# Stick-breaking logits that alternate between two heads, and cross-attention values in four strips of 128 columns

## The chip, the cores and the metric

The kernel runs on one core of a Trainium2 chip. The metric is the device time of one execution in microseconds (us); less is better. The time of the kernel before is the median of three runs, 981.52 us.

## The reference, cut to what matters

One step of a small streaming encoder with two layers, 256 prompt tokens and 32 sample tokens, 1024 features, 16 heads of 64. Layer 0 mixes eight heads of softmax attention with eight heads of stick-breaking attention; layer 1 has sixteen softmax heads with a forget bias. Each layer then has a cross-attention into 256 memory tokens (4 heads of 256) and a SwiGLU feed-forward part. The change touches the stick-breaking logits and the cross-attention of the sample tokens.

```python
def stick_break_attend(q, k, v, q_pos, k_pos):
    z = jnp.einsum('bqhd,bkhd->bhqk', q, k).astype(jnp.float32) * (HEAD_DIM ** -0.5)
    before = k_pos[None, :] < q_pos[:, None]
    log_keep = jnp.where(before, jax.nn.log_sigmoid(-z), 0.0)
    log_later = lax.cumsum(log_keep, axis=3, reverse=True) - log_keep
    w = jnp.where(before, jnp.exp(jax.nn.log_sigmoid(z) + log_later), 0.0)
    return jnp.einsum('bhqk,bkhd->bqhd', w.astype(v.dtype), v)

def memory_attn(h, mk, mv, w_q, w_o):
    b, t, _ = h.shape
    q = (h @ w_q).reshape(b, t, XA_HEADS, XA_HEAD_DIM)
    s = jnp.einsum('bqhd,bkhd->bhqk', q, mk).astype(jnp.float32) * (XA_HEAD_DIM ** -0.5)
    p = jax.nn.softmax(s, axis=-1)
    o = jnp.einsum('bhqk,bkhd->bqhd', p.astype(mv.dtype), mv)
    return o.reshape(b, t, D_MODEL) @ w_o
```

## The kernel before

All activations stand with features on the 128 partitions and the 288 tokens (256 prompt, 32 sample) in the columns. A weight unit is a 128x1024 block (512 KB). `unit` (L132) loads it from HBM through SP's queue into `st`, makes a high part `hi` on ACT (L141) and the rest `lo` on DVE (L142), and `mm3` (L145) does three TensorE matmuls per 128x128 block with them: 24 per unit. `st` and `lo` have four buffers, `hi` five. These projections (`pj`, `op`, `dn`, `mv` in the trace) fill most of the time.

Attention is written as Python generators. `tick` (L176) advances each active one by a step after every projection, so that the pieces of attention lie between projections on TensorE, and the work of ACT and DVE for them runs beside the next projection. PSUM has four banks for accumulators of projections and four for attention (`att`, L64), each a bank of 128x512 fp32. An engine's instructions run mostly in the order of the source; at some places the framework has set a matmul of one piece between those of another.

The array has 128 rows (the contraction) and 128 columns (the output's partitions). A matmul whose operands stand on partitions 64 to 127 uses the lower row half, one whose output stands on PSUM partitions 32 to 63 the second strip of 32 columns. In the trace, a shape such as 64*128 gives rows and columns of the array that are used; a matmul of two plain fp32 operands leaves two records, its two passes.

The parts that the change touches:

- `stick_prompt` (L459), called for j = 4 to 7 in layer 0. A tile q[j] holds two heads, one in each half of the partitions. For head 0 and then head 1 it computes the logits `zb` in a PSUM bank of the head's own: two q.k matmuls with 64 rows (256 and 128 columns), then two full-array bf16 matmuls of `identb` with `mdiag`, which add the mask. `stick_logs` (L429) takes both banks through Abs, Exp and Ln on ACT and one DVE instruction per head. Three steps later `stick_weights` (L444) multiplies by `ntrir` and `nones` into the same banks.
- `stick_sample` (L480), called twice, for the 32 sample tokens of two tiles: for each head two matmuls with the cache's keys (`ck`, 64 rows, 128 columns of the array), one mask matmul (`msamp`), and two with the new keys (64 rows, 32 columns), into the head's bank `zs`.
- `attend` in `cross` (L626), called twice per layer by `sample` (L621), each time for two of the four heads: logits `xss`, softmax, two transposes `xst`, a DVE copy to `xsw`; then the values `xso`: for two halves kt of the memory and two heads i, a matmul with 32 columns of weights and 256 columns of values, head i on partitions 32i to 32i + 31. DVE copies 64x256 to `xsn`, two transposes of 64x128 put features on the partitions (`xsp`), and four `split_o` (L324; ACT, then DVE) write the output's parts `oh` and `ol`.
- For comparison: `attend_prompt` (L357) computes its logits `sc` for two heads from two row halves, with no mask matmul between; `sample_pv` (L407) computes `os` in four strips of 32 columns.
- Around them: `mem_scales` (L510) runs in the first `Memory.step` (L540) behind the first stick-breaking prompt call: matmuls `nrm`, then the chain on DVE that ends in `y` (L225 to L230), then matmuls `nr`. `head` (L598) is the cross-attention of the prompt (`xs`, `xt`, `xw`, `xo`), and `out_project` (L292) runs the output projection, in which the products that need the last heads come last.

Of the kernel before, what the change touches and what calls it, by code (L numbers as in the profile page):

```python
# [26 lines left out]
def encoder_step(ctx: ExitStack, tc: tile.TileContext, a):  # L27
# [14 lines left out]
    V, S, G, T, DMA = nc.vector, nc.scalar, nc.gpsimd, nc.tensor, nc.sync  # L42
    cnt = [0]

    def name(s):
        cnt[0] += 1
        return f"{s}{cnt[0]}"

    def tok(s, dt=F32):
        return tk.tile([P, NT], dt, tag="t", name=name(s))  # L50

    def work(s):
        return wk.tile([P, 512], F32, tag="w", name=name(s))

    def work2(s, dt=F32):
        return wk.tile([P, 768], dt, tag="w2", bufs=4, name=name(s))
# [7 lines left out]
    def att(s):  # L64
        return ps.tile([P, 512], F32, tag="at", bufs=4, name=name(s))

    def mm(out, lhsT, rhs, start=True, stop=True):
        T.matmul(out, lhsT, rhs, start=start, stop=stop, skip_group_check=True)  # L68
# [54 lines left out]
    ident = cst.tile([P, P], F32, name="ident")  # L123
# [189 lines left out]
    def split(t, hi, lo, eng=G):  # L313
        S.copy(hi, t)
        eng.tensor_tensor(lo, t, hi.bitcast(F32), ALU.subtract)
        return hi, lo
# [7 lines left out]
    def split_o(p, oh, ol):  # L324
        S.copy(oh, p)
        V.tensor_tensor(ol, p, oh.bitcast(F32), ALU.subtract)

    def v_natural(v):
        p = att("vt")
        T.transpose(p[:, 0:128], v[:, 0:128], ident)  # L330
        T.transpose(p[:, 128:256], v[:, 128:256], ident)
        T.transpose(p[0:NS, 256:384], v[:, 256:288], ident)
        vn = wk.tile([P, 384], F32, tag="vn", bufs=5, name=name("vn"))
        S.copy(vn[:, 0:256], p[:, 0:256])
        S.copy(vn[0:NS, 256:384], p[0:NS, 256:384])
        return vn
# [92 lines left out]
    def stick_logs(zs):  # L429

        ab = work2("ab")
        c = 0
        for z, n, _ in zs:
            S.activation(ab[:, c:c + n], z[:, :n], AF.Abs)
            c += n
        S.activation(ab[:, :c], ab[:, :c], AF.Exp, scale=-1.0)
        S.activation(ab[:, :c], ab[:, :c], AF.Ln, bias=1.0)
        c = 0
        for z, n, _ in zs:
            V.scalar_tensor_tensor(ab[:, c:c + n], z[:, :n], 0.0, ab[:, c:c + n], op0=ALU.max, op1=ALU.add)  # L440
            c += n
        return ab

    def stick_weights(zs, sp, parts=None):  # L444

        w = work2("sw")
        c = 0
        for z, n, later in zs:
            if parts:
                mm(z[:, :n], ntrir, parts[0][:, c:c + n], False, False)  # L450
                mm(z[:, :n], ntrir, parts[1][:, c:c + n], False, False)
            else:
                mm(z[:, :n], ntri, sp[:, c:c + n], False, False)
            mm(z[:, later[0]:later[1]], nones, sp[:, c + later[2]:c + later[3]], False, True)
            S.activation(w[:, c:c + n], z[:, :n], AF.Exp)
            c += n
        return w

    def stick_prompt(q, k, v, vns, j, oh, ol):  # L459
        vn = vns[j] = v_natural(v)  # L460
        zs = []
        for hd in range(2):
            r = slice(64 * hd, 64 * hd + 64)
            z = att("zb")

            mm(z[:, 0:256], k[r, 0:128], q[r, 0:256], True, False)
            mm(z[:, 256:384], k[r, 128:256], q[r, 128:256], False, False)
            mm(z[:, 0:128], identb, mdiag, False, False)
            mm(z[:, 256:384], identb, mdiag, False, False)
            zs.append((z, 384, (128, 256, 256, 384)))  # L470
        sp = stick_logs(zs)
        parts = split(sp, work2("sh", F32R), work2("sl", F32R), V)
        yield 1
        yield 1
        yield 1
        w = stick_weights(zs, sp, parts)
        yield 1
        prompt_pv([w[:, 0:384], w[:, 384:768]], vn, oh, ol)

    def stick_sample(qs, ks, two, vns, ck, cv, o):  # L480
        yield 1

        zs = []
        for hd in range(2):
            z = att("zs")
            r = slice(64 * hd, 64 * hd + 64)
            for j in range(2):
                mm(z[:, 32 * j:32 * j + 32], ck[j][r], qs[j][r, 256:288], j == 0, False)
            mm(z[:, 64:128], identb, msamp, False, False)
            for j in range(2):  # L490
                mm(z[0:NS, 64 + 32 * j:96 + 32 * j], ks[j][r, 256:288], qs[j][r, 256:288], False, False)
            zs.append((z, 128, (0, 64, 64, 128)))
        sp = stick_logs(zs)
        yield 1
        yield 1
        w = stick_weights(zs, sp)
        yield 1
        yield from sample_pv(w, lambda j, hd: (128 * hd + 32 * j, 128 * hd + 64 + 32 * j), [vns[j] for j in two], cv, o)
# [74 lines left out]
    def cross(layer, cur, memory, nxt):  # L573
        o = ([tok("oh", F32R) for _ in range(KT)], [tok("ol", F32R) for _ in range(KT)])
        q, qs = [], []
# [50 lines left out]
        def attend(g, ck, cv):  # L626
            s = att("xss")
            for i in range(2):
                for f in range(2):
                    mm(s[32 * i:32 * i + 32, 0:256], qs[4 * g + 2 * i + f][:, 256:288], ck[i][:, 256 * f:256 * f + 256], f == 0, f == 1)  # L630
            e = work("xse")
            softmax(s[0:64], [(0, 256)], None, e[0:64])
            yield 1
            tt = att("xst")
            T.transpose(tt[:, 0:64], e[0:64, 0:128], ident[0:64, 0:64])
            T.transpose(tt[:, 64:128], e[0:64, 128:256], ident[0:64, 0:64])
            w = work("xsw")
            V.tensor_copy(w[:, 0:128], tt[:, 0:128])
            yield 1
            po = att("xso")  # L640
            for kt in range(2):
                for i in range(2):
                    mm(po[32 * i:32 * i + 32, 0:256], w[:, 64 * kt + 32 * i:64 * kt + 32 * i + 32],
                       cv[i][:, 256 * kt:256 * kt + 256], kt == 0, kt == 1)
            t = work("xsn")
            V.tensor_copy(t[0:64, 0:256], po[0:64, 0:256])
            yield 1
            pt = att("xsp")
            for f in range(2):
                T.transpose(pt[:, 64 * f:64 * f + 64], t[0:64, 128 * f:128 * f + 128], ident[0:64, 0:64])  # L650
            for i in range(2):
                for f in range(2):
                    b = 4 * g + 2 * i + f
                    split_o(pt[:, 64 * f + 32 * i:64 * f + 32 * i + 32], o[0][b][:, 256:288], o[1][b][:, 256:288])

        for hd in range(4):
            project_q(hd)
# [288 lines left out]
    r = tok("rf")  # L946
# [87 lines left out]
```

## Time and profile before

| What | Value |
|---|---|
| median of three runs | 981.52 us (979.58 to 983.31) |
| the profiled execution | 981.77 us, of which its span is 979.9 us |
| TensorE matmuls (PE) | 960.9 us busy, 98% of the span |
| weight loads (PEld) | 925.1 us, 94% |
| VectorE (DVE) | 589.5 us, 60% |
| ScalarE (ACT) | 483.8 us, 49% |
| GpSimd (POOL) | 194.6 us, 20% |
| chain of work that ended last | PE 90%, DMA 3%, DVE 3%, issue and ACT 1% each |

The span runs from the first to the last instruction that the profiler saw; the rest of the execution's time lies around it. Busy time of PE is to be read with care: a matmul's record lasts from its start to a modelled end, while the next has often started, so starts tell more than durations. A row of the timeline gives the start, the length from the first start to the last end of a run of like records, the engine, the line, the operation, the tile written and those read, the shape and the number of records. All matmuls but transposes are written by the helper in line 68, so they are told apart by their tiles.

### The profile page before, as it was taken

Reading aid. Unit: us, or ns where it says so; the run is one execution under the profiler, and the core shown is the slowest. Engines: PE = TensorE matmul, PEld = TensorE weight load, DVE = VectorE, ACT = ScalarE, POOL = GpSimd, SP = SyncE. Lnnn points to the kernel's source line nnn. Section 1 sums busy time; section 2 is a strip of 40 time slices with the busy share of each in tenths; the row PEclk is TensorE's granted clock in tenths of the full one; section 3 lists DMA queues with packets and bytes.
Section 4 is the critical chain, followed back from the end, with each engine's and each line's share of the span. In section 5 each row is a group of like instructions: output and inputs, shape, how many; then the busy total and the mean of one; then the engine's idle time right before and its main releaser. Section 6 shows DMA issues by size and latency. Waiting matters only on the chain.

```text
span 979.9 us, 19034 instructions
## 1 busy us (share of the span) xinstructions
PE 960.9 (98%) x7449; PEld 925.1 (94%) x7449; DVE 589.5 (60%) x1135; ACT 483.8 (49%) x854; POOL 194.6 (20%) x293
## 2 busy tenths in 40 slices
PE   8999999999999999999999999999999999999995
PEld 7789999998899999999998999999989999999995
DVE  6686454677676555764565666657757655555452
ACT  5556767555455444444444545445546544444330
POOL 3121001210113222411003234213002222222010
PEclk9999999999999999999999999999999999999997
DMA  7775345544254454455455555545425444444431
GB/s 235 247 248 192 127 165 174 169 168 143 91 179 158 165 173 167 178 193 173 166 201 167 179 191 182 170 160 194 149 100 168 155 159 165 173 164 166 165 109 49
DMA packets 60137, 163.59 MB, mean 167 GB/s; under 512 B 8160, under 2 KB 21520, under 8 KB 60048
## 3 DMA queue, kind: packets, MB, share of 16 engines
q1 hardware_dynamic: 60048, 162.38, 49.0%
q8 instruction: 59, 0.97, 0.4%
q14 instruction: 30, 0.25, 0.1%
HBM read 152.20 MB, written 11.72 MB: 167 GB/s over the span
## 4 chain that ended last, share of the span: by engine, by line
PE 90%; DMA 3%; DVE 3%; issue 1%; ACT 1%; SPq 0%; POOL 0%; DVEq 0%; ACTq 0%; POOLq 0%
PE pj L68 50%; PE dn L68 14%; PE op L68 11%; PE mv L68 5%; DMA st<-w_ab 2%; PE zb L68 1%; PE xs L68 1%; PE xo L68 1%; PE po L68 1%; DVE lo L142 1%; DMA skew<-lined 1%; PE sc L68 1%; PE nr L68 1%; ACT hi L141 1%; PE zs L68 1%
## 5 line engine op out<-in xcount | busy, mean ns | idle before, releaser
L141 ACT CAST hi<-st 128x1024 fp32r<-128x1024 f32 x260 | 272.2, 1049 | 339.4 <-issue 146.9
L68 PE MATMUL pj<-hh,hi 128*128 128x288 f32 (+1 forms) x1352 | 405.1, 300 | 0.0
L68 PE MATMUL pj<-hl,hi 128*128 128x288 f32 (+1 forms) x1352 | 399.8, 296 | 1.7 <-DVE hl L248 1.7
L142 DVE TENSOR_TENSOR lo<-st,hi 128x1024 fp32r<-128x1024 f32 x260 | 323.3, 1244 | 128.8 <-PE dn L68 41.3
L68 PE MATMUL pj<-hh,lo 128*128 128x288 f32 (+1 forms) x1352 | 399.4, 295 | 0.0
L68 PEld LDWEIGHTS pj<-hh,hi 128*128 128x128 f32 x1352 | 256.6, 190 | 6.2 <-issue 4.7
L68 PEld LDWEIGHTS pj<-hl,hi 128*128 128x128 f32 x1352 | 256.5, 190 | 3.3 <-DVE hl L248 3.2
L68 PEld LDWEIGHTS pj<-hh,lo 128*128 128x128 f32 x1352 | 256.7, 190 | 0.0
L68 PE MATMUL dn<-fh,hi 128*128 128x288 f32 x400 | 108.7, 295 | 0.0
L68 PE MATMUL dn<-fh,lo 128*128 128x288 f32 x352 | 103.7, 295 | 0.0
L68 PE MATMUL dn<-fl,hi 128*128 128x288 f32 x304 | 89.5, 294 | 0.0
L68 PE MATMUL op<-ol,hi 128*128 128x288 f32 x256 | 75.5, 296 | 0.0
L68 PE MATMUL op<-oh,lo 128*128 128x288 f32 x256 | 75.5, 295 | 0.0
L68 PE MATMUL op<-oh,hi 128*128 128x288 f32 x256 | 75.1, 296 | 0.0
L68 PEld LDWEIGHTS dn<-fh,hi 128*128 128x128 f32 x400 | 72.5, 188 | 0.0
L68 PEld LDWEIGHTS dn<-fh,lo 128*128 128x128 f32 x352 | 66.1, 188 | 0.0
L213 POOL TENSOR_TENSOR ssq<-ssq,sq 128x288 f32<-128x288 f32 (+1 forms) x37 | 37.0, 1000 | 120.0 <-ACT sq L202 77.8
L68 PEld LDWEIGHTS dn<-fl,hi 128*128 128x128 f32 x304 | 57.1, 188 | 0.0
L691 POOL TENSOR_TENSOR fl<-us,fh 128x288 fp32r<-128x288 f32 x38 | 32.8, 863 | 119.0 <-ACT fh L690 119.0
L686 DVE TENSOR_TENSOR us<-pj,rstd 128x288 f32<-128x288 f32 x44 | 20.1, 457 | 59.4 <-PE pj L68 59.4
L687 POOL TENSOR_TENSOR gs<-gs,sg 128x288 f32<-128x288 f32 x44 | 38.8, 882 | 75.5 <-ACT sg L685 75.5
L68 PEld LDWEIGHTS op<-ol,hi 128*128 128x128 f32 x256 | 48.2, 188 | 0.8 <-issue 0.8
(253 smaller groups left out, 1213.7 us busy)
## 6 DMA issues: line engine op xcount, KB each, us to landing
st<-w_gate SPq DMA_DIRECT2D x44, 512.0 KB, 3.3
st<-w_up SPq DMA_DIRECT2D x44, 512.0 KB, 3.2
st<-w_down SPq DMA_DIRECT2D x44, 512.0 KB, 3.3
st<-w_c SPq DMA_DIRECT2D x25, 512.0 KB, 3.3
st<-w_ab SPq DMA_DIRECT2D x23, 512.0 KB, 4.2
st<-w_xk SPq DMA_DIRECT2D x16, 512.0 KB, 3.6
st<-w_xv SPq DMA_DIRECT2D x16, 512.0 KB, 3.5
st<-w_xq SPq DMA_DIRECT2D x16, 512.0 KB, 4.3
```

Of the source, the lines that this page charges most:

```text
L68: T.matmul(out, lhsT, rhs, start=start, stop=stop, skip_group_check=True)
L141: S.copy(hi[:, b], st[:, b])
L142: V.tensor_tensor(lo[:, b], st[:, b], hi[:, b].bitcast(F32), ALU.subtract)
L213: eng.tensor_tensor(s[:, :self.n], self.acc[i][:, :self.n], q[:, :self.n], ALU.add)
L686: V.tensor_tensor(us, pu[:, :NT], cur.r, ALU.mult)
L687: G.tensor_tensor(gs, gs, sg, ALU.mult)
L691: G.tensor_tensor(lo, us, hi.bitcast(F32), ALU.subtract)
```

## The change

In `stick_prompt` both banks are taken first; the q.k matmuls go column block by column block and alternate between the two heads, which lie on the array's row halves; the mask matmuls of both heads follow. In `stick_sample` the same is done: the matmuls with the cache's keys alternate between the heads, then come both mask matmuls, then those with the new keys, alternating. In `attend` of the cross-attention the values of two heads are computed in four strips of 32 array columns, each with 128 columns of values (head i, half f of its features) where there were two with 256: 16 passes of 128 columns instead of 8 of 256. The copy to `xsn` covers 128x128 instead of 64x256, and one transpose of 128x128 takes the place of two of 64x128. The four `split_o` and their sizes stay.

```diff
--- before.py
+++ after.py
@@ -458,16 +458,17 @@
 
     def stick_prompt(q, k, v, vns, j, oh, ol):
         vn = vns[j] = v_natural(v)
-        zs = []
-        for hd in range(2):
-            r = slice(64 * hd, 64 * hd + 64)
-            z = att("zb")
-
-            mm(z[:, 0:256], k[r, 0:128], q[r, 0:256], True, False)
-            mm(z[:, 256:384], k[r, 128:256], q[r, 128:256], False, False)
+        zz = [att("zb") for _ in range(2)]
+
+
+        for k0, q0, c0, c1 in ((0, 0, 0, 256), (128, 128, 256, 384)):
+            for hd in range(2):
+                r = slice(64 * hd, 64 * hd + 64)
+                mm(zz[hd][:, c0:c1], k[r, k0:k0 + 128], q[r, q0:256], k0 == 0, False)
+        for z in zz:
             mm(z[:, 0:128], identb, mdiag, False, False)
             mm(z[:, 256:384], identb, mdiag, False, False)
-            zs.append((z, 384, (128, 256, 256, 384)))
+        zs = [(z, 384, (128, 256, 256, 384)) for z in zz]
         sp = stick_logs(zs)
         parts = split(sp, work2("sh", F32R), work2("sl", F32R), V)
         yield 1
@@ -480,16 +481,17 @@
     def stick_sample(qs, ks, two, vns, ck, cv, o):
         yield 1
 
-        zs = []
-        for hd in range(2):
-            z = att("zs")
-            r = slice(64 * hd, 64 * hd + 64)
-            for j in range(2):
+        zz = [att("zs") for _ in range(2)]
+        rr = [slice(64 * hd, 64 * hd + 64) for hd in range(2)]
+        for j in range(2):
+            for z, r in zip(zz, rr):
                 mm(z[:, 32 * j:32 * j + 32], ck[j][r], qs[j][r, 256:288], j == 0, False)
+        for z in zz:
             mm(z[:, 64:128], identb, msamp, False, False)
-            for j in range(2):
+        for j in range(2):
+            for z, r in zip(zz, rr):
                 mm(z[0:NS, 64 + 32 * j:96 + 32 * j], ks[j][r, 256:288], qs[j][r, 256:288], False, False)
-            zs.append((z, 128, (0, 64, 64, 128)))
+        zs = [(z, 128, (0, 64, 64, 128)) for z in zz]
         sp = stick_logs(zs)
         yield 1
         yield 1
@@ -638,20 +640,20 @@
             V.tensor_copy(w[:, 0:128], tt[:, 0:128])
             yield 1
             po = att("xso")
+
+            strips = [(i, f, slice(64 * i + 32 * f, 64 * i + 32 * f + 32)) for i in range(2) for f in range(2)]
             for kt in range(2):
-                for i in range(2):
-                    mm(po[32 * i:32 * i + 32, 0:256], w[:, 64 * kt + 32 * i:64 * kt + 32 * i + 32],
-                       cv[i][:, 256 * kt:256 * kt + 256], kt == 0, kt == 1)
+                for i, f, b in strips:
+                    mm(po[b, 0:128], w[:, 64 * kt + 32 * i:64 * kt + 32 * i + 32],
+                       cv[i][:, 256 * kt + 128 * f:256 * kt + 128 * f + 128], kt == 0, kt == 1)
             t = work("xsn")
-            V.tensor_copy(t[0:64, 0:256], po[0:64, 0:256])
+            V.tensor_copy(t[:, 0:128], po[:, 0:128])
             yield 1
             pt = att("xsp")
-            for f in range(2):
-                T.transpose(pt[:, 64 * f:64 * f + 64], t[0:64, 128 * f:128 * f + 128], ident[0:64, 0:64])
-            for i in range(2):
-                for f in range(2):
-                    b = 4 * g + 2 * i + f
-                    split_o(pt[:, 64 * f + 32 * i:64 * f + 32 * i + 32], o[0][b][:, 256:288], o[1][b][:, 256:288])
+            T.transpose(pt[:, 0:128], t[:, 0:128], ident)
+            for i, f, b in strips:
+                m = 4 * g + 2 * i + f
+                split_o(pt[:, b], o[0][m][:, 256:288], o[1][m][:, 256:288])
 
         for hd in range(4):
             project_q(hd)
```

## Rows read from the trace of the kernel before

**Rows 1.** Windows: busy us (instructions) by PE, PEld, DVE, ACT, POOL; clock, DMA.
```profile
84.00:264.00 180.00, 179.86 (x1407) 168.78 (x1406) 106.73 (x204) 108.60 (x194) 20.50 (x22) 1.00 0.44 148
690.00:738.00 48.00, 48.00 (x361) 42.83 (x361) 30.25 (x72) 22.30 (x56) 1.54 (x2) 1.00 0.31 110
```

**Rows 2.** ACT's groups, 84 to 264 us: busy, mean ns | idle before, its releasers.
```profile
L141 ACT CAST hi<-st 128x1024 fp32r<-128x1024 f32 x42 | 43.9, 1047 | 51.5 <-PE pj L68 23.9 <-issue 8.9 <-PE op L68 8.4
```

**Rows 3.** Timeline of PE, first stick-breaking prompt call: start, length (us), instruction.
```profile
84.53 0.27 PE L331 MATMUL vt<-ident,kv 128*128 128x128 f32 x1
84.64 0.27 PE L332 MATMUL vt<-ident,kv 128*32 128x128 f32 x1
84.84 0.92 PE L68 MATMUL zb<-q,kv 64*128 64x256 f32 x4
85.69 0.28 PE L68 MATMUL zb<-mdiag,identb 128*128 128x128 bf16 x2
...
86.76 0.28 PE L68 MATMUL zb<-mdiag,identb 128*128 128x128 bf16 x2
86.88 0.56 PE L68 MATMUL nrm<-mean,ssq 128*128 128x2 f32 x4
```

**Rows 4.** Timeline of PE, logits of a softmax prompt call, both heads.
```profile
27.61 0.93 PE L68 MATMUL sc<-kv,q 64*128 64x128 f32 x8
28.47 0.40 PE L68 MATMUL pj<-hh,hi 128*128 128x288 f32 x1
```

**Rows 5.** Timeline of PE, first stick-breaking sample call, from head 0 to head 1.
```profile
111.07 0.63 PE L68 MATMUL zs<-q,ca 64*128 64x32 f32 x4
111.64 0.20 PE L68 MATMUL zs<-msamp,identb 128*128 128x64 bf16 x1
...
112.01 0.63 PE L68 MATMUL zs<-q,ca 64*128 64x32 f32 x4
```

**Rows 6.** Timeline of PE, values of the cross-attention's first sample.
```profile
233.36 1.06 PE L68 MATMUL xso<-ca,xsw 128*32 128x256 f32 x8
234.35 0.40 PE L68 MATMUL pj<-hh,hi 128*128 128x288 f32 x1
```

**Rows 7.** Timeline of PE, values of a softmax sample in four strips.
```profile
53.16 0.32 PE L68 MATMUL os<-ca,pts 128*32 128x64 f32 x8
53.41 0.31 PE L68 MATMUL os<-vn,pts 32*32 32x64 f32 x8
```

**Rows 8.** Timeline of PE around the transposes of the cross-attention's first sample.
```profile
238.71 0.40 PE L68 MATMUL xo<-xw,vh 128*128 128x256 f32 x2
238.95 0.28 PE L68 MATMUL xo<-xw,vl 128*128 128x256 f32 x1
239.16 0.33 PE L650 MATMUL xsp<-ident,xsn 64*128 64x64 f32 x2
...
239.64 0.29 PE L68 MATMUL xs<-kl,qh 128*128 128x256 f32 x1
```

**Rows 9.** Timelines of DVE, ACT and PE behind the first prompt call.
```profile
86.61 0.19 DVE L326 TENSOR_TENSOR ol<-ot,oh 128x32 fp32r<-128x32 f32 x1 [0.84 <-ACT oh L325]
87.48 0.16 DVE L225 TENSOR_SCALAR ms<-nrm 128x4 f32<-128x4 f32 x1 [0.67 <-PE nrm L68]
...
87.08 0.49 ACT L434 ACTIVATE ab<-zb 128x384 f32<-128x384 f32 x1 [0.50 <-PE zb L68]
...
89.67 0.71 PE L68 MATMUL nr<-ident,y 128*128 128x128 f32 x4
```

**Rows 10.** Timelines of DVE and PE, second sample call: its logs made and used.
```profile
161.34 0.49 DVE L440 SCALAR_TENSOR_TENSOR ab<-zs,ab 128x128 f32<-128x128 f32 x2 [2.19 <-ACT ab L437]
...
163.31 0.39 PE L68 MATMUL zs<-ab,ntri 128*128 128x128 f32 x2
```

**Rows 11.** Timelines of DVE and PE, end of the first cross-attention.
```profile
257.26 0.69 DVE L326 TENSOR_TENSOR xw<-xt,xw 128x512 fp32r<-128x512 f32 x1 [1.59 <-ACT xw L325]
...
258.61 0.28 PE L68 MATMUL xo<-xw,vh 128*128 128x256 f32 x1
```

## What the change does to the time: the prediction

> **What bounds the kernel now.** I read the busy time by stretch first. In the 180 us that hold all stick-breaking work and the first cross-attention, TensorE (PE) is busy 179.86 us, and in the second cross-attention 48.00 of 48 us; VectorE (DVE) and ScalarE (ACT) stay near 60%, the DMA engines at 0.44 and 0.31 [rows 1]. So here a microsecond that PE does not spend is a microsecond off the end, unless something else comes due. The nearest candidate is the weights, each cast on ACT into a high part (`hi`) before PE can use it. Most of the idle time that ACT has before these casts (23.9 + 8.4 of 51.5 us) ends with PE's own matmuls, which free the buffers [rows 2]: the weights wait for PE, not PE for them. That leaves the order of PE's matmuls, read from PE's timeline, start to start, since the ends in the trace are modelled.
>
> **Stick-breaking logits of the prompt** (4 calls, heads j = 4 to 7). Today head 0's four q·k passes (two matmuls in fp32, two passes each) start at 84.84, its two mask matmuls with `identb` at 85.69, head 1's mask matmuls at 86.76, the next work at 86.88 [rows 3]. That is 2.04 us, of which one head's q·k passes take 0.85. Where a matmul uses another part of the array than the one before, the start comes late: from the last transpose `vt` to the first `zb` 0.20 us, where two transposes are 0.11 apart [rows 3]. Softmax attention has passes of the same two shapes for two heads, with no mask matmul between the heads: all 8 start from 27.61, and the next work at 28.47, 0.86 us [rows 4]. Two heads cost there what one costs in `zb`, so the row halves run beside each other, and what keeps them apart in `zb` is the full-array mask matmul. The edit takes it out of the way. After it I expect 0.86 for both heads and 4 mask matmuls at the 0.12 per pair of the last pair [rows 3]: 1.10 instead of 2.04, **-0.94** each, -3.76 in four calls. Lower bound if nothing overlaps: passes in turn for 2 x 0.63 us of streaming (0.21 for 256 columns and 0.11 for 128, two passes each), once the 0.22 around them, and the masks 0.24, 1.73: -0.31. I take the first end, since the row has the same shapes.
>
> **Stick-breaking logits of the sample** (2 calls). One head takes 0.94 us: 0.57 for the cache part, 0.37 for the mask and the new keys [rows 5]. After the edit both heads take that once, plus one more mask pass (0.06, half the pair of [rows 3]) and some 0.03 for the second half's starts: 1.03 instead of 1.88, **-0.85**, -1.70 in two calls. Without overlap the second head's cache passes (0.11 apart: four take 0.44) and new keys (0.12) come on top: -0.30.
>
> **Values of the cross-attention's sample** (4 calls, two per layer). Now 8 passes of 256 columns in two strips take 0.99 us [rows 6]; the nearest work in four strips, `os`, takes 0.25 for 8 passes of 64 columns [rows 7]. With two strips side by side the first streams 4 x 256 = 1024 columns, with four the second 2 x 64 = 128. The difference is 0.74 us per 896 columns, 0.83 ns a column, and 0.14 stays as a fixed part. The changed form, 16 passes of 128 columns in four strips, streams 4 x 128 = 512: 0.14 + 0.42 = 0.57, **-0.42**, -1.69 in four calls. At the other end, strips in pairs only, it stays at 0.99. The `os` row has four strips with different data in each, so I take the first.
>
> **Turning the values back.** Two transposes of 64 rows become one of 128. Now `xo`'s last pass starts at 238.95 and the second pass of `xs` at 239.64, 0.69 us with two changes of shape [rows 8]. With a full-array transpose there is none: one `xo` pass (0.12: two of them lie between 238.71 and 238.95), one transpose (0.11, [rows 3]) and one `xs` pass (0.12), 0.35: **-0.34**, -1.38 in four calls. The DVE copy before it goes from 64x256 to 128x128, half the columns, and isn't on the chain; the four casts after it are unchanged. No DMA and no weight is moved, so SP's and POOL's queues stay as they are.
>
> The savings add up to 3.76 + 1.70 + 1.69 + 1.38 = **8.5 us**.
>
> **What is late next.** (1) Between the first prompt call and the memory's scales: PE issues `nrm`, DVE makes `y` from `ms` on, and PE's `nr` at 89.67 follows it at once. `nrm` moves 0.94 earlier, but DVE's `ms` (87.48) stands behind `ol` (86.61, done at 86.80), and that behind ACT's work on head 0's logits, which does not move [rows 9]. `ms` can move by 0.68 only: 0.26 given back, once. (2) The sample's `ab` is done on DVE at 161.34 + 0.49 = 161.83, and PE uses it at 163.31 [rows 10]: 1.48 to spare. PE comes 0.94 + 0.85 = 1.79 earlier; ACT's chain starts some 0.5 earlier too, since it idled 0.50 for head 1's logits [rows 9] and now finds both. 0.2 is left; were the chain not earlier, PE would wait 0.3 at this place. I take 0.1. (3) At the end of each cross-attention `xo` follows the split `xw`, which ends at 257.26 + 0.69 = 257.95, while PE starts on it at 258.61 [rows 11]: 0.66 to spare, of which the values take 0.42. Behind it the late products of the output projection wait for the casts of the turned values, with 0.34 less PE work ahead of them. I have no row for their margin, so between nothing and 0.34 in each of two layers; I take 0.2. Together 0.26 + 0.1 + 0.4 = 0.8 given back. What PE loses when it waits delays nothing else: ACT and DVE queue behind it with idle time to spare.
>
> **The sum.** -8.5 + 0.8 = -7.7. The profiled execution took 981.77 us, of which its span is 979.9; the edits lie inside the span. 981.77 - 7.7 = 974.1; the median of the three runs is 0.25 lower, so 973.8. I say **974.0**, -0.8%.
>
> **Rivals.** *A, the saved time turns into waits.* PE arrives earlier at results that others make and waits there. The price is bounded, as a wait ends at the latest where PE now stands: all gains of the two stick samples and of the prompt calls before them (2 x 1.79), of the last sample in each layer (2 x 0.76), and 0.26, together 5.4 of 8.5, 978.7. For it: the spare 0.2 in (2). Against it: that needs the ACT and DVE chains not to move at all, and they start with PE. *B, nothing overlaps.* The lower ends give 4 x 0.31 + 2 x 0.30 + 0 + 1.38 = 3.2, less 0.5 of waits: 979.1. Against it stand 0.86 for two heads and 0.25 for four strips [rows 4, 7]. *C, passes start strictly in the order written*, both passes of a head's matmul before the other head's, so that only neighbours overlap. A prompt call then streams 0.85 instead of 0.63 (-0.73 left), a sample's logits lose 0.14 (-0.71), and in the values each strip's second pass waits for its first, so that four strips need 9 steps of 0.11 instead of 4: 0.53 more, which turns -0.42 into +0.11. In all -2.9 - 1.4 + 0.4 - 1.4 = -5.3, with 0.5 given back 977.0. Against it: in [rows 4] the code writes all of head 0 before head 1, and in that order the 8 passes could hardly overlap at all, yet they end in 0.86. The Trainium skill, "TensorE: Matmul & The Clock Gate" (Part 3, Packing small matmuls, "What overlaps and what doesn't"), states just this rule: matmuls start and end in program order, without reordering. By that page rival C would be the forecast; the trace disagrees with it by its 0.86, so it keeps a small chance. *D, slower: a change of row half or strip costs what a change of shape costs.* Around `xsp` two such changes cost the 0.34 between 0.69 and 0.35 [rows 8], 0.17 each. The new order has 3 changes of half per prompt call, 6 per sample call and 7 changes of strip per values call, 52 in all. Against B's saving of 3.2 stand 52 x 0.17 = 8.8, so 5.6 us slower, 987.4. It decides from 0.06 us per change on (3.2 / 52). Against it: four strips with 8 passes in 0.25 us [rows 7] leave 0.03 for each pass altogether. The Trainium skill, "TensorEngine Tiling (Array Packing)" (Key Properties), also says that a change of tiling mode drains the engine, and not a change of tile; by it, D's price would be zero, and the 0.25 agrees.
>
> **How the numbers follow.** Forecast 0.79, A 0.07, B 0.05, C 0.05, D 0.04. About 0.5% (4.9 us) is what a measurement of this kernel can tell from no change, so faster means under 976.6. The forecast lies there; A, B and C (978.7, 979.1, 977.0) are within, D is slower: 0.79, 0.17, 0.04. The range: all savings with nothing given back is 973.0, the three runs before spread by some 1.8 to either side, so 971.5 at the bottom; at the top it takes in A, B and C, 979.5.
>
> **What would show it.** In the changed profile, a prompt call's `zb` should take 1.10 us from its first pass to the next work, with the mask matmuls at its end; a sample's `zs` 1.03; `xso` 0.57 with starts in groups of four; one `xsp` transpose of 128x128 without a pause around it. PE should still be busy all through both stretches. Waits of PE on `ab`, `sl`, `xw` or `oh` there of over 2 us in all would mean A; `zb` at 1.3 and `xso` near 1.1 would mean C; at 1.7 and 1.0, B. I am wrong if those blocks shrink as told and the end doesn't follow: then the weights, or a chain that I hold for covered, set the pace.

## The result, and the profile after

The changed kernel takes **973.26 us** (median, 972.87 to 974.63), the kernel before beside it 981.63 us: a ratio of 0.9919, 95% interval 0.9901 to 0.9937. The forecast was 974.0. The profiled execution took 973.61 us, of which its span is 971.8.

First the two stretches that bounded the kernel before, by windows (columns as in [rows 1]), of the changed kernel:

```profile
84.00:264.00 180.00, 179.82 (x1473) 171.27 (x1472) 112.66 (x212) 113.53 (x203) 23.92 (x24) 1.00 0.47 155
690.00:738.00 48.00, 47.94 (x384) 44.74 (x384) 32.59 (x71) 24.42 (x59) 5.16 (x5) 1.00 0.37 126
```

TensorE (PE) is as full as in [rows 1], at the same granted clock of 1.00, and the end has come forward by 8.1 us of span: the time came out of PE's own order, and no other engine took PE's place as the bound.

Next the four edits in PE's timeline of the changed kernel (start, length, engine, line, operation, output and inputs, rows and columns of the array that are used, shape, count): the first two prompt calls, a sample's logits, the values, and the turning back.

```profile
85.16 0.92 PE L68 MATMUL zb<-q,kv 64*128 64x256 f32 x8
86.02 0.40 PE L68 MATMUL zb<-mdiag,identb 128*128 128x128 bf16 x4
86.29 0.61 PE L68 MATMUL nrm<-mean,ssq 128*128 128x2 f32 x4
...
105.48 0.92 PE L68 MATMUL zb<-q,kv 64*128 64x256 f32 x8
106.34 0.40 PE L68 MATMUL zb<-mdiag,identb 128*128 128x128 bf16 x4
106.54 0.36 PE L68 MATMUL pj<-hh,hi 128*128 128x256 f32 x1
...
109.36 0.28 PE L68 MATMUL pj<-hh,lo 128*128 128x256 f32 x1
109.57 0.64 PE L68 MATMUL zs<-q,ca 64*128 64x32 f32 x8
...
110.54 0.40 PE L68 MATMUL pj<-hh,hi 128*128 128x288 f32 x1
...
228.22 0.64 PE L68 MATMUL xso<-ca,xsw 128*32 128x128 f32 x16
228.79 0.40 PE L68 MATMUL pj<-hh,hi 128*128 128x288 f32 x1
...
233.37 0.28 PE L68 MATMUL xo<-xw,vl 128*128 128x256 f32 x1
233.49 0.27 PE L653 MATMUL xsp<-ident,xsn 128*128 128x128 f32 x1
...
233.72 0.28 PE L68 MATMUL xs<-kl,qh 128*128 128x256 f32 x1
```

What the reader is to see: where [rows 3] has two heads one behind the other, eight passes now start at 85.16 and the four mask passes of both heads at 86.02, 0.86 us behind them, just as in [rows 4]. From first start to next work the call takes 86.29 - 85.16 = 1.13 us (2.04 before), the second one 106.54 - 105.48 = 1.06. A sample's logits take 110.54 - 109.57 = 0.97 ([rows 5] shows 0.94 for one head), the values 228.79 - 228.22 = 0.57 ([rows 6]: 0.99), and from `xo`'s last pass to the second pass of `xs` it is 233.72 - 233.37 = 0.35 ([rows 8]: 0.69).

Every block of that kind, start to start, in us:

| Block | before | after | difference | forecast |
|---|---|---|---|---|
| `zb`, 4 calls | 2.04, 2.01 x3 | 1.13, 1.06 x3 | -0.91, -0.95 x3: **-3.76** | -3.76 |
| `zs`, 2 calls | 1.86 x2 | 0.97 x2 | -0.89 x2: **-1.78** | -1.70 |
| `xso`, first call of each layer | 0.99 x2 | 0.57 x2 | -0.41 x2 | -0.42 x2 |
| `xso`, second call of each layer | 0.55 + 0.98 | 0.34 + 0.57 | -0.63, -0.62 | -0.42 x2 |
| `xo`'s last pass to the second pass of the next work, 4 calls | 0.69 x2, 0.71 x2 | 0.35 x2, 0.36 x2 | -0.35 x4: **-1.39** | -1.38 |

With -2.07 for the values this is -9.0 us. Against before, PE stood 0.32 us later at the first `zb` and 5.20 earlier behind the last stick-breaking work (177 us); 5.14 earlier ahead of the first cross-attention and 6.47 behind it; 6.76 and 8.10 at the second. So the three stretches that hold the edit shrank by 5.52, 1.33 and 1.34, 8.19 in all; 0.8 to 0.9 was given back inside them (below).

### The profile page after: what moved, and what is told of

Its sections match the earlier page's. It is cut to its first block, busy times and chain, and to the rows that moved or that the text cites. A ratio compares the mean times of both kernels' runs of the same rounds, so it can differ in the third digit from the quotient of the medians.

```text
span 971.8 us, 19089 instructions
## 1 busy us (share of the span) xinstructions
PE 951.7 (98%) x7477; PEld 919.4 (95%) x7477; DVE 588.5 (61%) x1135; ACT 483.6 (50%) x854; POOL 195.9 (20%) x293
## 4 chain that ended last, share of the span: by engine, by line
PE 91%; DVE 3%; DMA 2%; issue 1%; ACT 1%; SPq 0%; POOL 0%; DVEq 0%; ACTq 0%; POOLq 0%
PE pj L68 51%; PE dn L68 14%; PE op L68 11%; PE mv L68 5%; DMA st<-w_ab 1%; PE xo L68 1%; PE po L68 1%; PE xs L68 1%; PE zb L68 1%; DVE lo L142 1%; PE sc L68 1%; PE nr L68 1%; PE nrm L68 1%; PE xss L68 1%; DMA x<-xT 0%
## 6 DMA issues: line engine op xcount, KB each, us to landing
st<-w_gate SPq DMA_DIRECT2D x44, 512.0 KB, 3.3
st<-w_up SPq DMA_DIRECT2D x44, 512.0 KB, 3.2
st<-w_down SPq DMA_DIRECT2D x44, 512.0 KB, 3.2
st<-w_c SPq DMA_DIRECT2D x25, 512.0 KB, 3.3
st<-w_ab SPq DMA_DIRECT2D x23, 512.0 KB, 4.3
st<-w_xk SPq DMA_DIRECT2D x16, 512.0 KB, 3.5
st<-w_xv SPq DMA_DIRECT2D x16, 512.0 KB, 3.4
st<-w_xq SPq DMA_DIRECT2D x16, 512.0 KB, 4.2
```

## The experiments

All kernels compute the whole result. Each is timed beside the kernel before on its chip.

**e1_stick_only** has the two stick-breaking functions of the changed kernel and the cross-attention of the one before; **e2_cross_only** has the two the other way round. They ask whether the parts add up or get into each other's way.

> Both stick-breaking functions as in the changed kernel, the cross-attention as before. My theory (each block's saving passes to the end in full): the trace of the changed kernel gives 4 prompt blocks 3.76 us and 2 sample blocks 1.78 us less, so 981.6 - 5.5 = 976.1. Rival (savings of the two halves cover each other's waits, so one alone brings less, or the time came from elsewhere): 978 or more.

> The cross-attention as in the changed kernel, the stick-breaking functions as before. My theory: values 2 x 0.41 + 2 x 0.63 and turning back 4 x 0.33 us less, 0.35 given back in two waits at xt and 0.3 in op rows: 981.6 - 2.7 = 978.9, and the wait at xt of 0.17 appears in both layers again, since it comes from this half alone. Rival (the wait at xt comes with the earlier arrival from the stick-breaking part): no such wait here.

Measured: e1 975.95 us, ratio 0.9933 (0.9918 to 0.9948), e2 979.77 us, ratio 0.9971 (0.9959 to 0.9982). The blocks are those of the changed kernel where the edit is in, and those of before where it is not (`zb` 1.13 and 1.06 in e1, `xso` 0.57 in e2). The product, 0.9904, lies within the interval of both edits together: the parts add up, and two thirds of the gain is the stick-breaking part.

**e3_head_outer** writes all passes of head 0 before those of head 1, masks last, in the prompt's and the sample's logits; **e4_strip_outer** writes both halves of the memory for one strip before the next strip. If passes started strictly as written (rival C), both would lose most of the overlap.

```diff
-        for k0, q0, c0, c1 in ((0, 0, 0, 256), (128, 128, 256, 384)):
-            for hd in range(2):
-                r = slice(64 * hd, 64 * hd + 64)
+        for hd in range(2):
+            r = slice(64 * hd, 64 * hd + 64)
+            for k0, q0, c0, c1 in ((0, 0, 0, 256), (128, 128, 256, 384)):
...
```

```diff
-            for kt in range(2):
-                for i, f, b in strips:
+            for i, f, b in strips:
+                for kt in range(2):
```

> The changed kernel, but the logits of both stick-breaking functions written head by head, masks still behind both heads. My theory (what separated the heads was the full-array mask matmul; the order of the halves is indifferent): prompt blocks stay at 1.06 to 1.13 us, sample blocks at 0.97, the end at 973.3. Rival (passes start strictly as written, so alternation makes the overlap): 0.2 to 0.6 us more per prompt block, 0.1 to 0.4 per sample block, the end at 974.3 to 976.5.

> The changed kernel, but the values of the cross-attention's sample are written strip by strip: four passes for one strip before the next strip's, so that the first pass of the last strip stands twelve places behind the first. My theory (the engine starts a pass as soon as its strip is free, also ahead of waiting ones): xso stays at 0.57 us per call, the end at 973.3. Rival (passes start in the order written, only neighbours overlap): 13 steps of 0.11 us, 1.5 us per call, 0.97 more, the end near 977.

Measured: e3 974.08 us, ratio 0.9911 (0.9897 to 0.9926), e4 973.95 us, ratio 0.9905 (0.9888 to 0.9921). The second prompt call in PE's timeline of e3:

```profile
104.57 0.93 PE L68 MATMUL zb<-q,kv 64*128 64x256 f32 x8
...
105.64 0.36 PE L68 MATMUL pj<-hh,hi 128*128 128x256 f32 x1
```

and the values in that of e4:

```profile
228.12 0.66 PE L68 MATMUL xso<-ca,xsw 128*32 128x128 f32 x16
228.72 0.40 PE L68 MATMUL pj<-hh,hi 128*128 128x288 f32 x1
```

1.07 us against 1.06 (a sample's logits 0.99 against 0.97), and 0.59 against 0.57 (228.122 to 228.716 unrounded). In e4 a strip's own four passes are written one after the other and would start 0.11 apart (128 columns each), so that in the written order the last of 16 could start only 4 x 3 x 0.11 = 1.3 us behind the first. Still the 16 start in four groups, in 0.39 us. The trace does not name the strip of a pass, but four passes of one strip in one group would be 512 columns in 0.11 us, the time of one full-array transpose of 128 columns [rows 3]. In e3 the shapes show directly which passes start first. By tile, `zb` in e3 from 104.50 to 104.95 us:

```profile
L68 PE MATMUL zb<-q,kv x4: 376/428/480, 104.6 to 104.9; 64*128 64x256 f32 x4
```

These are the first four starts, and all have 256 columns, so they are two passes of each head; the passes of 128 columns follow from 105.11 on. As written, head 0's two passes of 128 columns stand ahead of head 1's first pass. The framework did not simply set both kernels in one order: in e3 and e4 the starts of a pair or group lie 13 to 14 ns apart, in the changed kernel 6 to 7. **Rival C falls**: what lies on another half or strip starts ahead of what is written before it. The order that the diff writes out between heads is not what brings the gain; that the mask matmuls no longer stand between them is.

**e5_mask_between** keeps the alternation and puts the mask matmuls of a column block behind that block, so that a prompt call has two changes of shape more.

```diff
                 mm(zz[hd][:, c0:c1], k[r, k0:k0 + 128], q[r, q0:256], k0 == 0, False)
-        for z in zz:
-            mm(z[:, 0:128], identb, mdiag, False, False)
-            mm(z[:, 256:384], identb, mdiag, False, False)
+            for z in zz:
+                mm(z[:, c0:c0 + 128], identb, mdiag, False, False)
```

> The changed kernel, but each column block of the prompt's logits is followed by its two mask matmuls: the heads still alternate, with two more changes of the array's shape per call and the same passes. My theory (a change of shape costs some 0.17 us): each prompt block 0.3 us longer, 1.4 instead of 1.1, the end 1.2 us later, 974.5. Rival (alternation alone makes the gain): blocks stay at 1.1, the end at 973.3.

Measured: 974.59 us, ratio 0.9915 (0.9899 to 0.9932). The second prompt call in PE's timeline of e5:

```profile
105.61 0.70 PE L68 MATMUL zb<-q,kv 64*128 64x256 f32 x4
106.24 0.29 PE L68 MATMUL zb<-mdiag,identb 128*128 128x128 bf16 x2
106.46 0.49 PE L68 MATMUL zb<-q,kv 64*128 64x128 f32 x4
...
106.97 0.36 PE L68 MATMUL pj<-hh,hi 128*128 128x256 f32 x1
```

1.37 us (106.974 - 105.607 unrounded) instead of 1.06, with the same 12 passes: 0.31 for two changes between 64 rows and the full array, **0.15 each**. A call of the kernel before has as many changes as one of e5 and takes 2.01 us. So of the 0.95 us that a call gained, 0.64 (2.01 to 1.37) is the two heads running beside each other, and 0.31 the two changes of shape that go. The end time doesn't resolve 4 x 0.3 us.

**e7_turn_halves** asks the same of the turning back: two transposes of 64 rows, one on each row half, in banks of their own, where the changed kernel has one of 128.

```diff
-            pt = att("xsp")
-            T.transpose(pt[:, 0:128], t[:, 0:128], ident)
+            pt = [att("xsp") for _ in range(2)]
+            for i in range(2):
+                r = slice(64 * i, 64 * i + 64)
+                T.transpose(pt[i][:, 0:64], t[r, 0:128], ident[r, r])
...
```

> The changed kernel, but the values are turned back by two transposes of 64 rows, one per row half, each into a bank of its own, as a shape of 64 rows again. My theory (what the one transpose saves is two changes of shape): from xo's last pass to the second pass of xs 0.6 us instead of 0.35, 0.25 to 0.35 more per call, the end 1.0 to 1.4 us later, 974.5. Rival (the saving was the number of transposes): two that overlap cost what one costs, no change.

Measured: 975.34 us, ratio 0.9924 (0.9909 to 0.9938). PE's timeline of e7 at the place of [rows 8]:

```profile
234.67 0.28 PE L68 MATMUL xo<-xw,vl 128*128 128x256 f32 x1
234.87 0.28 PE L655 MATMUL xsp<-ident,xsn 64*128 64x64 f32 x2
...
235.30 0.29 PE L68 MATMUL xs<-kl,qh 128*128 128x256 f32 x1
```

From `xo`'s last pass to the second of `xs` 0.63 us, where [rows 8] gives 0.69 and the changed kernel 0.35. That the two transposes run beside each other brings 0.06; the full-array shape brings the other 0.28. So nearly all of this term is the two changes of shape that go.

Little of it reaches the end, though. From the first `xss` of a layer to the first `pj` behind its output projection (216.96 to 275.48 us in layer 0 of the changed kernel) it is 58.52 and 58.57 us in the changed kernel, 59.82 and 59.88 before, and in e7 58.58 and 58.69: 0.18 more in both layers together, where the four blocks are 4 x 0.28 = 1.1 us longer. The waits that the changed kernel has behind its turning back (points 3 and 4 of the next section) are not there in e7, whose products run at an even 0.13 and whose `xt` starts 0.12 behind the pass before it. That e7's time came out 1.4 to 1.7 us above e4 and e6 on the same chip is therefore not shown to come from the edit: in its profiled execution the first `zb` already starts at 86.47 us (85.16 in the changed kernel), behind a fall of the granted clock at 34 us.

**e6_mask_first** turns this into an edit: the sample's mask matmuls go to the front, next to the full-array work before them, so that a call has three changes of shape in place of four.

```diff
+        for z in zz:
+            mm(z[:, 64:128], identb, msamp, True, False)
         for j in range(2):
             for z, r in zip(zz, rr):
-                mm(z[:, 32 * j:32 * j + 32], ck[j][r], qs[j][r, 256:288], j == 0, False)
-        for z in zz:
-            mm(z[:, 64:128], identb, msamp, False, False)
+                mm(z[:, 32 * j:32 * j + 32], ck[j][r], qs[j][r, 256:288], False, False)
```

> The changed kernel, but the sample's mask matmuls come first, in the full array as the work before them, so that the block has three changes of shape instead of four. My theory (each change costs 0.1 to 0.2 us): zs 0.80 to 0.87 us per call instead of 0.97, the end 0.2 to 0.35 us earlier, 973.0. Rival (the changes are hidden by loads): zs stays at 0.97.

Measured: 973.62 us, ratio 0.9906 (0.9891 to 0.9920): not to be told from the changed kernel. PE's timeline of e6:

```profile
109.19 0.28 PE L68 MATMUL pj<-hh,lo 128*128 128x256 f32 x1
109.31 0.23 PE L68 MATMUL zs<-msamp,identb 128*128 128x64 bf16 x2
109.47 0.64 PE L68 MATMUL zs<-q,ca 64*128 64x32 f32 x8
...
110.28 0.40 PE L68 MATMUL pj<-hh,hi 128*128 128x288 f32 x1
```

The block itself, first start to next work, stays at 0.97 us, and read so, the theory falls. But the change that is gone lay in front of the block: from the last projection to the next it is 110.28 - 109.19 = 1.09 us, against 110.54 - 109.36 = 1.18 in the changed kernel. That is 0.09 per call, the same in the second call (1.19 to 1.09), and less than the 0.15 of e5: the price of a change depends on the passes on both sides. The masks now follow the projection at its own pace (109.19 to 109.31). Of the three changes left, those behind the narrow masks and behind the new keys start 0.12 us after the pass before them, the one behind the cache's keys 0.20.

**e8_fewer_shapes** adds to e6 the transposes `xst` of the cross-attention's sample: full-array, with the rows that are not used set to zero on POOL beforehand.

```diff
+            G.memset(e[64:128, 0:256], 0.0)
...
-            T.transpose(tt[:, 0:64], e[0:64, 0:128], ident[0:64, 0:64])
-            T.transpose(tt[:, 64:128], e[0:64, 128:256], ident[0:64, 0:64])
+            T.transpose(tt[:, 0:128], e[:, 0:128], ident)
+            T.transpose(tt[:, 128:256], e[:, 128:256], ident)
...
```

> The changed kernel with the sample's mask first and, in the cross-attention, the two transposes of the sample's weights (64 rows) done in the full array (the unused rows set to zero on POOL), 128 columns each. My theory: each of the four calls loses two changes of shape (0.34) and gains 0.11 us of streaming, 0.24 less; with 0.1 to 0.17 for each of two sample blocks 1.2 to 1.3 us less in all, 972.0. Rival (waits at xt and xo take it back, as 0.17 was taken per layer): 973.

Measured: 972.48 us, ratio 0.9898 (0.9884 to 0.9913). In PE's timeline of e8,

```profile
223.96 0.29 PE L68 MATMUL xs<-kh,ql 128*128 128x256 f32 x1
224.08 0.27 PE L638 MATMUL xst<-ident,xse 128*128 128x128 f32 x1
...
224.44 0.29 PE L68 MATMUL pj<-hl,hi 128*128 128x288 f32 x1
```

the last `xs` pass and the second projection are 0.48 us apart; in the changed kernel it is 0.71 (223.93 to 224.64). Against that, the first two passes of each second `xso` call take 0.13 more (0.34 to 0.47). With e6's part that makes 4 x 0.23 - 2 x 0.13 + 2 x 0.09 = 0.8 us by blocks. By the same two stretches as for e7 it is less: 58.29 and 58.44 us against 58.52 and 58.57, so 0.36 for the transposes, and with 0.18 for the logits 0.54. Part of what the blocks save is waited for again. To see whether this holds against the changed kernel itself, both ran again on one chip, with the kernel before for its trace:

> The changed kernel once more, to read two things of the trace that are not of the edit's own blocks. The layer-0 feed-forward projections (982 pj matmuls in a row) took 129.65 us in the kernel before and 130.43 in the changed one, and the stretch near 515 us held 3.4 us at half the granted clock in the kernel before and none in the changed one. Theory K, both belong to the kernel: 130.4 again and no dip near 515. Theory X, both belong to the execution: either may come out otherwise, 129.6 to 130.4, and a dip of some 1.5 us may show anywhere. Both theories have the time at 973 to 974, the edit's blocks as in the first trace (zb 1.13 and 1.06, zs 0.97, xso 0.57).

> The changed kernel with the sample's mask matmuls first and the transposes of the cross-attention's sample made full-array (the rows that are not used set to zero on POOL), once more, beside the changed kernel on one chip. By the changes of shape that it saves (0.1 in each of two zs calls, 0.1 to 0.15 net in each of four xst) it should be 0.5 to 0.8 us under the changed kernel; the rival has it equal, as what is saved in front of a wait is waited for instead. More than 0.5 us between the medians speaks for the first, under 0.2 for the second.

> The kernel before once more, for its trace alone. Theory K (the 129.65 us of the layer-0 feed-forward projections and the dip of the granted clock near 515 us belong to the kernel): both again. Theory X (they belong to the execution): the projections anywhere from 129.6 to 130.4, the dip at another place or none. The blocks of the edit should stand as in the first trace, zb at 2.0, zs at 1.87, xso at 0.99.

Measured: the changed kernel 974.53 us (973.04 to 975.15), ratio 0.9920 (0.9905 to 0.9935); e10, which is e8, 974.01 us (972.93 to 974.81), ratio 0.9919 (0.9903 to 0.9934); the kernel before 981.91 in its profiled execution. The medians differ by 0.52 us the expected way, but each kernel's executions spread by some 2 us. **That e8 is shorter than the changed kernel is seen in its stretches, not in its time**: against e9, e10's two stretches are 58.31 and 58.45 us to 58.55 and 58.59, which with 0.17 in the logits makes 0.55, after 0.54 in the first pair of traces.

The other question of these three was about PE's tempo outside the edit. One window of each of the four traces, first of before, then of e11 (before again):

```profile
515.00:521.00 6.00, 6.00 (x39) 6.00 (x39) 2.46 (x6) 2.26 (x4) 1.46 (x2) 0.72 0.46 128
```

```profile
527.00:533.00 6.00, 4.66 (x23) 4.36 (x24) 3.49 (x12) 2.78 (x7) 0.18 (x1) 0.73 0.28 79
```

then after and e9 (after again):

```profile
515.00:521.00 6.00, 5.99 (x46) 5.22 (x45) 2.27 (x6) 3.21 (x7) 2.49 (x7) 1.00 0.70 235
```

```profile
508.00:514.00 6.00, 6.00 (x39) 5.54 (x37) 2.81 (x6) 1.76 (x3) 1.47 (x2) 0.72 0.45 135
```

The granted clock (the third number from the right) falls to half, the lower of its two levels (1.2 GHz), for 3.4 us: from 515.5 us in one execution of the kernel before and from 529.8 in the other, where 515 to 521 is at 1.00; from 509.7 in one execution of the changed kernel, and in the other not at all between 18 and 960 us. Each of the three falls comes behind a wait of PE of 1.4 to 1.9 us (starting at 512.0, 526.3 and 506.3); the execution without a fall has such waits too (1.4 us at 506.2, 2.2 at 520.7). So this fall belongs to the execution, not to the kernel. (At the start all four run at the lower level, their products 0.24 us apart instead of 0.13, up to 15 to 18 us; the traces have no record of the clock before its first rise, and a window shows 1.00 there.) The long run of 982 projections in layer 0, on the other hand, took 129.65 and 129.66 us in the two traces of the kernel before (293.05 to 422.70 in the first, 292.79 to 422.45 in the second) and 130.43 and 130.44 in the two of the changed kernel (286.57 to 417.01 in the first): 0.8 ns more per matmul, spread over all of them, at a granted clock of 1.00. This belongs to the kernel.

## Why the prediction was right, point by point

**The bound.** Right: PE stayed full in both stretches, the blocks shrank, and the end followed. (ACT near 60% holds for the first stretch of [rows 1]; in the second it was 22.30 of 48 us, 46%.)

**Logits of the prompt.** Forecast -3.76, measured -3.76. The row that carried it, two heads in 0.86 us in softmax attention, came out to the hundredth (85.16 to 86.02). The masks took 0.27 in the first call and 0.20 in the others (106.34 to 106.54), against the 0.24 of two pairs.

**Logits of the sample.** -1.70 forecast, -1.78 measured: the second mask pass starts 0.04 us behind the first, where 0.06 was allowed, and the second half's starts lie 6 to 7 ns behind the first's in the records, less than the 0.03 in all that was allowed for them.

**Values.** 0.57 was forecast from a line through two rows, and 0.57 it is. Mis-sized is the sum, -1.69 against -2.07, as the term took all four calls for one block. In the second call of each layer the framework has set the first matmul, two passes, between the transposes `xt` of another piece. Before, in PE's timeline:

```profile
255.46 0.62 PE L68 MATMUL xso<-ca,xsw 128*32 128x256 f32 x2
256.01 0.55 PE L610 MATMUL xt<-ident,xe 128*128 128x128 f32 x3
256.48 1.05 PE L68 MATMUL xso<-ca,xsw 128*32 128x256 f32 x6
257.46 0.40 PE L68 MATMUL op<-ol,hi 128*128 128x288 f32 x1
```

and after:

```profile
249.71 0.41 PE L68 MATMUL xso<-ca,xsw 128*32 128x128 f32 x2
250.04 0.55 PE L612 MATMUL xt<-ident,xe 128*128 128x128 f32 x3
250.52 0.64 PE L68 MATMUL xso<-ca,xsw 128*32 128x128 f32 x14
251.09 0.40 PE L68 MATMUL op<-ol,hi 128*128 128x288 f32 x1
```

The lone first matmul pays for its 256 columns by itself (0.55 us with the change of shape), and with 128 only 0.34: 0.21 more per layer than forecast. The rows of before showed this split, and it was not looked at.

**Turning back.** -1.38 forecast, -1.39 measured, and e7 shows that it is the change of shape, as was said. As a gain of the end it was overrated: most of it is waited for again at (3) and (4) below, and e7, without this gain, is only 0.18 us longer over both stretches.

**What was given back.** 0.8 forecast, some 0.9 measured, from partly other places. (1) At the memory's scales 0.26 was expected and 0.05 came. The forecast had DVE's `ms` stand behind `ol`, and that behind ACT's work on head 0's logits, as in [rows 9]. In the changed kernel ACT's cast `oh` stands ahead of those logits:

```profile
86.14 0.17 ACT L325 CAST oh<-ot 128x32 fp32r<-128x32 f32 x1
86.34 0.87 ACT L434 ACTIVATE ab<-zb 128x384 f32<-128x384 f32 x2
```

and DVE, in its own timeline, done with `ol` at 86.35 + 0.19 = 86.54, waits for `nrm` itself:

```profile
86.35 0.19 DVE L326 TENSOR_TENSOR ol<-ot,oh 128x32 fp32r<-128x32 f32 x1 [0.25 <-ACT oh L325]
86.93 0.16 DVE L225 TENSOR_SCALAR ms<-nrm 128x4 f32<-128x4 f32 x1 [0.39 <-PE nrm L68]
```

From `nrm` to `nr` it is 89.13 - 86.29 = 2.84 us, 2.79 before. The step that failed was to keep an engine's order from the old trace, though the framework sets it anew. (2) At the sample's `ab` 0.1 was allowed and nothing came: it is done at 157.45 + 0.49 = 157.94, PE uses it at 158.12. Of the 1.48 us of [rows 10], 0.18 is left; forecast 0.2. (3) At the late products of the output projection 0.4 was expected in both layers and about 0.45 came (0.26 and 0.19). In PE's timeline of the changed kernel, layer 0:

```profile
254.87 0.40 PE L68 MATMUL op<-ol,hi 128*128 128x288 f32 x1
255.10 0.29 PE L68 MATMUL op<-oh,lo 128*128 128x288 f32 x1
255.26 0.41 PE L68 MATMUL op<-oh,hi 128*128 128x288 f32 x1
255.50 0.30 PE L68 MATMUL op<-ol,hi 128*128 128x288 f32 x1
```

Starts that are 0.13 apart elsewhere lie 0.24, 0.16 and 0.24 apart here (unrounded), and the casts come just ahead: DVE's `ol<-xsp` ends at 254.63 + 0.18 = 254.81, ACT's `oh<-xsp` at 255.02 + 0.19 = 255.21. Before, the same products ran at an even 0.13. The two casts, DVE's and then ACT's, in their timelines of the changed kernel:

```profile
254.63 0.18 DVE L326 TENSOR_TENSOR ol<-xsp,oh 128x32 fp32r<-128x32 f32 x1
```

```profile
255.02 0.19 ACT L325 CAST oh<-xsp 128x32 fp32r<-128x32 f32 x1
```

(4) Not foreseen: 0.17 and 0.19 at the next head's transposes `xt`, one in each layer. DVE's `xe` is made behind the casts of the turned values:

```profile
237.70 0.62 DVE L353 TENSOR_SCALAR xe<-xe,st 128x256 f32<-128x256 f32 x2
```

PE's last projection before it starts at 237.87, `xt` only at 238.20, 0.33 later; before these two were 0.16 apart (243.80, 243.96). PE's turning back got 0.34 shorter, and the chain of casts did not. e2 has the same wait (0.32 and 0.36 from the pass before to `xt`), e1 has not (0.17 and 0.15), so it comes from the cross-attention's edit alone. In the sum the blocks gained 0.5 more than forecast, 0.4 of it at `xso`; (3) and (4) gave back 0.4 more than was allowed, (1) and (2) 0.3 less. So -7.7 became -8.1.

**The end.** -9.0 + 0.05 + 0.45 + 0.36 = -8.1 by blocks, 8.19 by stretches; the profiled execution lost 8.16 (981.77 to 973.61). That this fits so well is partly luck. The 0.78 us of the projections in layer 0 were lost outside the edit, and the profiled execution of before held a fall of the granted clock, near 515 us, that cost about 1.5 us, of which PE's longer wait behind it (for DVE's `e`, 1.9 us at the longest after, 1.2 before) took 0.6 back. PE was also 0.3 later before the first `zb` (84.84 to 85.16). These add up to +0.2, so that some 0.3 stays unassigned.

**The rivals.** A (waits take it back) holds for 0.9 us, not for 5.4, and there mostly for one term, the turning back. B (nothing overlaps) falls with every block. C (strictly in written order) falls with e3 and e4. The Trainium skill, "TensorE: Matmul & The Clock Gate" (Part 3, Packing small matmuls, "What overlaps and what doesn't"), says that matmuls start and end in program order; here the measurement differs, 1.07 us with heads written one after the other against 1.06 alternating. D (a change of half or strip costs 0.17) falls too: 16 passes with a change of strip nearly each time take 0.57. A change of shape is what costs, 0.09 to 0.15 each in e6 and e5; the Trainium skill, "TensorEngine Tiling (Array Packing)" (Key Properties), says that a change of tiling mode drains the engine, and the trace agrees in that the starts behind such a change come late; the draining itself no run shows.

**What stays open.** Why the 982 projections take 0.8 ns longer each. All kernels with the changed stick-breaking functions have it (130.43 to 130.46 us) but e5, in which only the masks' place differs (129.80); those without don't (129.65 to 129.66). ACT, DVE and POOL do the same work in the same order there in both, and it was not tried further.

## What to carry to other kernels

Where small matmuls on different row halves or strips should run beside each other, look for a full-array matmul that stands between them, a mask or a transpose, and move it to the side where full-array work already is; the order among the small ones matters little. Price such an edit by a block of the same shapes elsewhere in the same trace, and count changes of shape on both sides of the block, not only inside it. When PE's part of a hand-over gets shorter, ask for the chains on other engines that start at the same point and did not: here they took back a tenth of the whole gain, and most of what the wider transpose had saved. So measure the stretch up to the next steady run as well as the block.

## What the runs showed of the hardware that was not expected

- PE starts passes ahead of others that are written before them, if they lie on another part of the array: in e4, 16 passes written strip by strip start in four groups of four, 13 to 14 ns apart within a group and 0.11 to 0.13 us from group to group.
- Passes on two row halves start 6 to 7 ns apart when the heads are written in turn (109.566 and 109.572 unrounded in `zs`), and 13 ns apart when they are written one after the other (108.661 and 108.675 in e3).
- A change of shape has no fixed price: 0.15 us between 64 rows and full array around passes of 128 and 256 columns (e5), 0.14 at the transposes (e7), 0.09 in front of the sample's logits (e6).
- One and the same run of 982 projections has a tempo that repeats to 0.02 us from execution to execution of a kernel and differs by 0.6% between two kernels, while a fall of the granted clock to 0.5 for 3.4 us, behind a wait of PE of 1.4 to 1.9 us, comes in some executions of a kernel and not in others; the one near 515 us was worth 1.5 us of the end.
